# A hybrid decoder layer: POOL's arithmetic given to DVE, the scaling of attention weights to ACT

## The chip, the core and the metric

The kernel runs on one core of one Trainium2 chip. The core has a matrix engine (TensorE, in profiles PE, with its weight loads as PEld), two engines for elementwise work that matter here, VectorE (DVE) and GpSimd (POOL), one for functions and copies, ScalarE (ACT), and a sync engine (SP) whose queue issues the DMAs. The engines run at the same time, each works through its own list of instructions strictly in order, and they wait for each other by semaphores. PE writes its results to PSUM banks, which DVE and ACT read; everything else lies in SBUF, and weights, inputs and results in HBM. The metric is the device time of one execution in microseconds (us).

## What is computed

One layer of a decoder (model width 1024) for a prompt of 2048 positions and 8 sample rows of one position each, which share all weights. In short:

```python
h = rms_norm(x, norm1_w);  proj = h @ w_in
q, k, v, z, xbc, dt_raw = split(proj)
a     = sliding_window_attention(q, k, v, sinks, rel_bias)      # window 128, 8 heads, 2 key/value heads
s_out = ssm_mixer(z, xbc, dt_raw, ...)                          # convolution, chunked state scan, gate, norm
x = x + concatenate([a, s_out]) @ w_out
h2 = rms_norm(x, norm2_w)
x = x + (silu(h2 @ w_gate) * (h2 @ w_up)) @ w_down              # hidden width 2816
y = rms_norm(x, final_norm_w)
```

Attention weights are `e / (sum(e) + exp(sink - m))`, computed in blocks of 128 queries against 256 keys. The scan works in chunks of 128 positions and carries a state of 8 heads x 64 x 128. New keys, values, convolution rows and states are outputs too.

## The kernel before

**Groups.** The 2048 + 8 columns are worked in six groups of 2, 3, 3, 3, 3 and 2 blocks of 128 (the last with the 8 sample rows), that is with 256, 384 or 264 columns. Activations stand with features on partitions, so a matmul has a weight tile of 128 x 128 and 256 to 384 moving columns.

**Pairs.** Every matmul of a projection is done three times to keep float32's precision: a number is split into a rounded half `hi` and a remainder `lo`, and `mm3` (L104 inside `mm`) adds hi*hi, hi*lo and lo*hi. Of activations, ACT makes `hi` by a copy, and DVE or POOL the remainder by a subtraction (L339 in `scaled`, L921 in `stage_s`, L1009 in `hid2`, L554 and L482 for keys and values).

**Weights.** `weight` (L210 and around) brings a weight piece of 128 x 512 (for the down projection mostly 128 x 384). The first times it is loaded raw (L206 into `wraw`, four buffers), ACT rounds it (L207), and DVE and POOL by turns subtract (L210); the pair lies in one of five `w2` buffers. At a first, second or third use, spread over the pieces, the pair is written to HBM (L214), and later uses load it whole (L203). So raw pieces, and with them L207 and L210, are frequent early and end around 1350 us.

**Stages.** Generators emit the work of a stage piece by piece: `stage_x0`/`stage_x` (load and first norm), `stage_a`, `stage_k`, `stage_b` (input projection, convolution), `stage_p` (attention), `stage_q` (state scan, `ssd`), `stage_y` (sample rows), `stage_s` (pairs of the mixed output), `stage_o` (output projection), `stage_h` (second norm), `stage_f` (feed-forward), `stage_z` (final norm, output). `run` advances a main stage and beside it others at set rates, so that the mixers of group i+1 are emitted among the feed-forward of group i. The tile framework then decides by an own estimate of every instruction's time, at build, in which order the instructions stand on each engine; buffers of a tag are taken in turn.

**POOL's work** in this kernel: half of the weight remainders (L210), the squares of the first group (L301), the sums of squares of the norms (`total`, L321), half of the activation remainders (L339, L921, L1009), all remainders of values (L482) and keys (L554), the scaling of attention weights by the inverse denominator (`scale`, L603), the triangular mask of one half (L626), the group sums (L673), three products of the scan (L742, L750, L757), the products and sums of the sample states (L893, L895), and small copies (L403, L407, L462 and others).

Of the kernel before, what the change touches and what calls it, by code (L numbers as in the profile page):

```python
# [31 lines left out]
NH = 8  # L32
# [40 lines left out]
def hymba(ctx: ExitStack, tc: tile.TileContext, I: dict, O: dict, groups):  # L73
# [125 lines left out]
    def weight(name, at, w=512):  # L199
        t = T([P, 1024], F32R, tag="w2", bufs=5)[:, :2 * w]  # L200
        hi, lo = t[:, :w], t[:, w:]
        if (name, at) in kept:
            SP.dma_start(t.bitcast(F32), kept[name, at])  # L203
            return hi, lo
        raw = T([P, 512], tag="wraw", bufs=4)[:, :w]
        SP.dma_start(raw, I[name][at] if name != "wd" else I[name][:, at:at + w])  # L206
        S.activation(hi, raw, AF.Copy)  # L207
        e = G if wn[0] % 2 else V
        wn[0] += 1
        e.tensor_tensor(lo, raw, hi.bitcast(F32), ALU.subtract)  # L210
# [70 lines left out]
    def stage_x0(g):  # L281
# [18 lines left out]
        for m in range(KT):  # L300
            G.tensor_tensor(xr[:, m, :N], xr[:, m, :N], xr[:, m, :N], ALU.mult)  # L301
            if m:
                V.tensor_tensor(xr[:, 0, :N] if m < KT - 1 else r, xr[:, 0, :N], xr[:, m, :N], ALU.add)
            if m % 4 == 3:
                yield
# [13 lines left out]

    def total(sq, t, N, e=G):  # L320
        e.tensor_tensor(sq[:, :N], sq[:, :N], t[:, :N], ALU.add)  # L321
# [11 lines left out]
    def scaled(x, c, r, N, pair, to):  # L333

        ts = {}

        def low(m):
            e = G if m % 2 else V
            e.tensor_tensor(pair[1][:, m, :N], ts[m], pair[0][:, m, :N].bitcast(F32), ALU.subtract)  # L339

        for m in range(KT + 2):
            if m >= 2:
                low(m - 2)
            if 1 <= m <= KT:
                S.activation(pair[0][:, m - 1, :N], ts[m - 1], AF.Copy)
            if m < KT:
                ts[m] = to(m)
                V.scalar_tensor_tensor(ts[m], x[:, m, :N], col(c, m), r[:, :N], ALU.mult, ALU.mult)  # L348
            yield
# [103 lines left out]
    def stage_k(g):  # L453
# [16 lines left out]
        def rows():  # L470
# [8 lines left out]
            for i, src in enumerate((vf[:, 0:nb], vd[:, :nb])):  # L479
                src = src.rearrange("p b (v c) -> p b v c", v=2)  # L480
                S.activation(vs[:, i, :nb, :, 0:64], src, AF.Copy)
                G.tensor_tensor(vs[:, i, :nb, :, 64:P], src, vs[:, i, :nb, :, 0:64].bitcast(F32), ALU.subtract)  # L482
            if last:
# [48 lines left out]
    def attention(g, b):  # L532
# [67 lines left out]
        def scale(kv):  # L600
            for r in range(4):
                h = kv * 4 + r
                G.tensor_scalar(sc[kv][:, r, 0:P], sc[kv][:, r, 0:P], rd[:, h:h + 1], 1.0, ALU.mult, ALU.mult)  # L603

# [11 lines left out]
        def finish(kv):  # L616
# [37 lines left out]
    def stage_q(g):  # L654
# [49 lines left out]
    def ssd(g, b):  # L704
# [68 lines left out]
    def stage_y(g):  # L773
# [111 lines left out]
        for i in range(NS):  # L885
# [6 lines left out]
            V.tensor_tensor(f4(xb), bb(bcb, 0), f4(dx[:, 1, :, i:i + 1].broadcast_to([P, 4, P])), ALU.mult)  # L892
            G.tensor_tensor(h, h, dx[:, 0, :, i:i + 1].broadcast_to([P, 4, P]), ALU.mult)  # L893
            yield
            G.tensor_tensor(h, h, xb, ALU.add)  # L895
            SP.dma_start(O["nss"][:, i], h)
# [15 lines left out]
    def stage_s(g):  # L912
# [6 lines left out]
        def low(t):  # L919
            e = G if t % 2 else V  # L920
            e.tensor_tensor(mix[1][:, t, :N], src[t], mix[0][:, t, :N].bitcast(F32), ALU.subtract)  # L921
# [28 lines left out]
    def norm_sum(g, x1, sq, m, N, n=1):  # L950
# [6 lines left out]
        def second():  # L957
            if m:
                total(sq, t[0], N, V if g is gs[-1] and n == 0 else G)
            g["nsq"] = g.get("nsq", 0) + 1  # L960
# [15 lines left out]
    def stage_f(g):  # L976
# [30 lines left out]
        def hid2(f, t, hh, hl):  # L1007
            e = G if f % 2 else V
            e.tensor_tensor(hl[:, 0, :N], t[:, :N], hh[:, 0, :N].bitcast(F32), ALU.subtract)  # L1009
# [214 lines left out]
```

## Time and profile before

| | |
|---|---|
| runs, us | 2434.94, 2443.29, 2444.47 (median 2443.29) |
| profiled execution, us | 2437.1, its span 2434.7 |
| mean granted clock of PE | 0.985 |
| busy in the span, us | PE 2314.5, weight loads 2244.4, DVE 1250.4, ACT 875.1, POOL 814.4 |
| DMA | 629 MB moved, 258 GB/s on average |

The profile is one execution; its times are of that execution alone. "Busy" is the time in which an engine had an instruction in work; PE's matmuls are pipelined, so that a busy PE need not be at its peak. A slice is a fortieth of the span (61 us), and a digit in it the busy share in tenths. A group of instructions is given as line, engine, operation, written and read tiles (buffer numbers left out), shape and count, then busy us and mean ns of one, then the idle time of the engine just before them and what ended it. A wait is given as who waited for whom, total us, times and longest. In a timeline row the first number is the start, the second the length.

### The profile page before, as it was taken

How to read it: one execution, taken by the hardware profiler on the slowest of the kernel's cores; microseconds unless marked ns; L12 is line 12 of the kernel's file. 1: busy time of each engine (PE TensorE's matmuls, PEld its weight loads, DVE VectorE, ACT ScalarE, POOL GpSimd, SP SyncE). 2: the span in 40 equal slices, each digit the busy share in tenths (PEclk: the TensorE clock that was granted, in tenths of full speed). 3: DMA queues.
4: the chain of work that ended last, by engine and by line, in shares of the span. 5: the costliest groups of instructions: out<-in, count | busy, mean ns of one | idle time of the engine just before them, and what ended most of it. 6: DMA issues, size and time to landing. Idle time of an engine off the chain costs nothing.

```text
span 2434.7 us, 39664 instructions
## 1 busy us (share of the span) xinstructions
PE 2314.5 (95%) x14633; PEld 2244.4 (92%) x14633; DVE 1250.4 (51%) x2526; ACT 875.1 (36%) x1861; POOL 814.4 (33%) x884
## 2 busy tenths in 40 slices
PE   6889898999999999999999999999999999999997
PEld 5779887889999999999999999999989999999997
DVE  8895978564556545344653533453354544233223
ACT  5665556454434434333432422132233212121001
POOL 5555766553444434223322312231123132111000
PEclk9899998999999999999999999999999999999999
DMA  8648575787776777878788887777789788888997
GB/s 276 221 151 284 186 239 195 248 306 272 252 247 212 243 246 278 272 262 277 242 281 285 269 250 243 238 215 240 237 308 301 230 280 270 249 294 306 332 339 259
DMA packets 227227, 628.97 MB, mean 258 GB/s; under 512 B 24323, under 2 KB 57916, under 8 KB 226892
## 3 DMA queue, kind: packets, MB, share of 16 engines
q1 hardware_dynamic: 226892, 626.26, 77.5%
q8 instruction: 116, 1.90, 0.3%
q14 instruction: 75, 0.61, 0.1%
q10 hardware_dynamic: 144, 0.20, 0.0%
HBM read 516.67 MB, written 110.21 MB: 257 GB/s over the span
## 4 chain that ended last, share of the span: by engine, by line
PE 68%; DMA 7%; DVE 2%; ACT 1%; issue 0%; SPq 0%; ACTq 0%; POOL 0%; DVEq 0%
PE psd L104 64%; PE psm L104 4%; DMA w<-wd 2%; DMA w<-wi 2%; DMA w<-wu 1%; DMA w<-wg 1%; DVE x L1042 1%; DVE xr L348 1%; DVE alo L339 0%; DMA out_yT_dram<-x 0%; DMA m<-sbcd 0%; PE psm L608 0%; PE psm L728 0%; DVE w L210 0%; ACT L696 0%
## 5 line engine op out<-in xcount | busy, mean ns | idle before, releaser
L104 PE MATMUL psd<-bhi,w 128*128 128x384 f32 (+1 forms) x4448 | 1097.4, 328 | 40.0 <-DVE w L210 14.9
L104 PEld LDWEIGHTS psd<-bhi,w 128*128 128x128 f32 x4448 | 785.6, 190 | 54.6 <-DVE w L210 19.1
L104 PE MATMUL psd<-blo,w 128*128 128x384 f32 (+1 forms) x2224 | 720.8, 324 | 0.7 <-DVE blo L339 0.6
L104 PE MATMUL psd<-hc,w 128*128 128x384 f32 (+2 forms) x3168 | 527.5, 323 | 28.6 <-DMA w<-wd 9.8
L104 PEld LDWEIGHTS psd<-hc,w 128*128 128x128 f32 x3168 | 502.5, 191 | 43.3 <-issue 12.4
L104 PE MATMUL psd<-ahi,w 128*128 128x384 f32 (+1 forms) x2272 | 516.7, 314 | 22.4 <-DMA w<-wi 8.4
L104 PEld LDWEIGHTS psd<-blo,w 128*128 128x128 f32 x2224 | 423.2, 190 | 2.8 <-DVE blo L339 1.1
L104 PEld LDWEIGHTS psd<-ahi,w 128*128 128x128 f32 x2272 | 386.1, 189 | 31.2 <-DMA w<-wi 5.0
L210 POOL TENSOR_TENSOR w<-wraw,w 128x512 fp32r<-128x512 f32 (+1 forms) x195 | 252.7, 1298 | 382.1 <-ACT w L207 346.3
L104 PE MATMUL psd<-alo,w 128*128 128x384 f32 (+1 forms) x1136 | 354.9, 312 | 0.0
L207 ACT ACTIVATE w<-wraw 128x512 fp32r<-128x512 f32 (+1 forms) x391 | 232.5, 601 | 324.4 <-PE psd L104 187.7
L994 DVE TENSOR_TENSOR x<-psd,x 128x384 f32<-128x384 f32 (+2 forms) x336 | 168.0, 510 | 193.9 <-PE psd L104 193.4
L104 PEld LDWEIGHTS psd<-alo,w 128*128 128x128 f32 x1136 | 215.2, 189 | 1.3
L210 DVE TENSOR_TENSOR w<-wraw,w 128x512 fp32r<-128x512 f32 (+1 forms) x196 | 164.4, 840 | 90.7 <-ACT w L207 88.6
L1009 POOL TENSOR_TENSOR hc<-tmp,hc 128x384 fp32r<-128x384 f32 (+2 forms) x66 | 67.6, 1025 | 356.8 <-ACT hc L1005 356.7
L1001 DVE SCALAR_TENSOR_TENSOR tmp<-tmp,psd 128x384 f32<-128x384 f32 (+2 forms) x132 | 66.7, 505 | 233.2 <-ACT tmp L1015 233.0
L1015 ACT ACTIVATE tmp<-psd 128x384 f32<-128x384 f32 (+2 forms) x132 | 59.7, 452 | 349.4 <-PE psd L104 349.2
L321 POOL TENSOR_TENSOR sq<-sq,tmp 128x384 f32<-128x384 f32 (+2 forms) x112 | 109.7, 979 | 199.4 <-ACT tmp L318 194.4
L1004 DVE SCALAR_TENSOR_TENSOR tmp<-psd,tmp 128x384 f32<-128x384 f32 (+2 forms) x132 | 67.4, 511 | 199.1 <-PE psd L104 198.8
L1005 ACT ACTIVATE hc<-tmp 128x384 fp32r<-128x384 f32 (+2 forms) x132 | 64.4, 488 | 270.4 <-DVE tmp L1004 267.0
L382 DVE SCALAR_TENSOR_TENSOR x<-tmp,cols,x 128x384 f32<-128x384 f32 (+1 forms) x144 | 100.3, 700 | 37.2 <-ACT x L404 26.7
L318 ACT ACTIVATE tmp<-x 128x384 f32<-128x384 f32 (+2 forms) x84 | 40.5, 489 | 137.5 <-DVE x L942 100.4
(269 smaller groups left out, 2145.3 us busy)
## 6 DMA issues: line engine op xcount, KB each, us to landing
w<-wu SPq DMA_DIRECT2D x177, 512.0 KB, 5.0
w<-wg SPq DMA_DIRECT2D x175, 512.0 KB, 4.5
w<-wi SPq DMA_DIRECT2D x144, 512.0 KB, 4.6
w<-wd SPq DMA_DIRECT2D x192, 384.0 KB, 3.8
w<-wo SPq DMA_DIRECT2D x65, 512.0 KB, 4.6
wraw<-in_wg_dram SPq DMA_DIRECT2D x89, 256.0 KB, 4.3
wu<-w SPq DMA_DIRECT2D x44, 512.0 KB, 3.3
wg<-w SPq DMA_DIRECT2D x44, 512.0 KB, 3.7
```

Source lines behind the costliest of these rows:

```text
L104: PE.matmul(o, l, r, start=start, stop=stop)
L207: S.activation(hi, raw, AF.Copy)
L210: e.tensor_tensor(lo, raw, hi.bitcast(F32), ALU.subtract)
L318: S.activation(t[:, :N], x[:, m, :N], AF.Square)
L321: e.tensor_tensor(sq[:, :N], sq[:, :N], t[:, :N], ALU.add)
L382: V.scalar_tensor_tensor(acc, raw[:, j:j + NP], cwc(j, t), acc, ALU.mult, ALU.add)
L994: V.tensor_tensor(x1[:, m, :N], p[:, :N], x1[:, m, :N], ALU.add)
L1001: V.scalar_tensor_tensor(t[:, :N], t[:, :N], 1.0, pg[:, :N], ALU.add, ALU.mult)
L1004: V.scalar_tensor_tensor(t[:, :N], pu[:, :N], 0.5, t[:, :N], ALU.mult, ALU.mult)
L1005: S.activation(hh[:, 0, :N], t[:, :N], AF.Copy)
L1009: e.tensor_tensor(hl[:, 0, :N], t[:, :N], hh[:, 0, :N].bitcast(F32), ALU.subtract)
L1015: S.activation(t[:, :N], pg[:, :N], AF.Tanh, scale=0.5)
```

## The change

All tensor_tensor instructions of POOL (G in the code: sums, differences and products) are issued on DVE (V) instead, with the same operands. Where the two engines took turns, DVE takes all. The scaling of the attention weights, four tensor_scalar instructions per key/value head, becomes four ACT copies with a scale per partition. POOL keeps its copies and memsets. One line falls away in `weight`, so that from there on the line numbers of the changed kernel are lower by one (L210 becomes L209).

```diff
 def weight(name, at, w=512):
         S.activation(hi, raw, AF.Copy)
-        e = G if wn[0] % 2 else V
-        wn[0] += 1
+        e = V
         e.tensor_tensor(lo, raw, hi.bitcast(F32), ALU.subtract)
...
 def stage_x0(g):
-            G.tensor_tensor(xr[:, m, :N], xr[:, m, :N], xr[:, m, :N], ALU.mult)
+            V.tensor_tensor(xr[:, m, :N], xr[:, m, :N], xr[:, m, :N], ALU.mult)
...
-    def total(sq, t, N, e=G):
+    def total(sq, t, N, e=V):
         e.tensor_tensor(sq[:, :N], sq[:, :N], t[:, :N], ALU.add)
...
         def low(m):
-            e = G if m % 2 else V
+            e = V
...
-                G.tensor_tensor(kl[r, kv, :W], kT[a, (b + k0) * P:(b + 2) * P], kh[a, kv, :W].bitcast(F32), ALU.subtract)
+                V.tensor_tensor(kl[r, kv, :W], kT[a, (b + k0) * P:(b + 2) * P], kh[a, kv, :W].bitcast(F32), ALU.subtract)
...
         def scale(kv):
             for r in range(4):
                 h = kv * 4 + r
-                G.tensor_scalar(sc[kv][:, r, 0:P], sc[kv][:, r, 0:P], rd[:, h:h + 1], 1.0, ALU.mult, ALU.mult)
+                S.activation(sc[kv][:, r, 0:P], sc[kv][:, r, 0:P], AF.Copy, scale=rd[:, h:h + 1])
...
-                G.tensor_tensor(as4(own[0]), as4(f32(ph)), tri4, ALU.mult)
+                V.tensor_tensor(as4(own[0]), as4(f32(ph)), tri4, ALU.mult)
...
-            G.tensor_tensor(s0[:, :N], s0[:, :N], s1[:, :N], ALU.add)
+            V.tensor_tensor(s0[:, :N], s0[:, :N], s1[:, :N], ALU.add)
...
 def ssd(g, b):
-        G.tensor_tensor(xdd, xdt, sm[:, 1, :].unsqueeze(2).broadcast_to([P, NH, 64]), ALU.mult)
+        V.tensor_tensor(xdd, xdt, sm[:, 1, :].unsqueeze(2).broadcast_to([P, NH, 64]), ALU.mult)
...
-        G.tensor_tensor(state, state, sm[:, 0, :].unsqueeze(2).broadcast_to([P, NH, 64]), ALU.mult)
+        V.tensor_tensor(state, state, sm[:, 0, :].unsqueeze(2).broadcast_to([P, NH, 64]), ALU.mult)
...
-            G.tensor_tensor(e, e, cb[:, q, :].unsqueeze(1).broadcast_to([P, 4, P]), ALU.mult)
+            V.tensor_tensor(e, e, cb[:, q, :].unsqueeze(1).broadcast_to([P, 4, P]), ALU.mult)
...
         def hid2(f, t, hh, hl):
-            e = G if f % 2 else V
+            e = V
```

Left out are the same replacement at L482, L893, L895, L921 and in `norm_sum`, where an exception for the last group becomes the rule.

The order of the instructions moves with it. Names in the rows carry buffer numbers, the last number being the tile's own.

First place: the first projection of the first group, where `blo` is the remainder of its input, `xr` the input that is squared (L301) and summed (L303), and `w2` a weight half out of `wraw`. Before, on DVE:

```order
L298 SCALAR_TENSOR_TENSOR blo_14_82<-xr_15_83,cols_4_68,bhi_13_81 128x256
L210 TENSOR_TENSOR w2_24_160<-wraw_25_161,w2_24_160 128x512
L303 TENSOR_TENSOR xr_15_83<-xr_15_83 128x256
L150 COPY m2_20_121<-psm_18_117 8x384
L475 COPY m2_128_702<-vp_11_77 128x128
L210 TENSOR_TENSOR w2_32_202<-wraw_33_203,w2_32_202 128x512
```

The second half of the first weight, w2_27_166, is not among these rows; it stands on POOL, between squares:

```order
L301 TENSOR_TENSOR xr_15_83<-xr_15_83 128x256 x7
L210 TENSOR_TENSOR w2_27_166<-wraw_28_167,w2_27_166 128x512
L301 TENSOR_TENSOR xr_15_83<-xr_15_83 128x256
L210 TENSOR_TENSOR w2_34_207<-wraw_35_208,w2_34_207 128x512
L210 TENSOR_TENSOR w2_40_247<-wraw_41_248,w2_40_247 128x512
```

Now, on DVE, from the same remainder on:

```order
L297 SCALAR_TENSOR_TENSOR blo_14_82<-xr_15_83,cols_4_68,bhi_13_81 128x256
L300 TENSOR_TENSOR xr_15_83<-xr_15_83 128x256
L209 TENSOR_TENSOR w2_24_160<-wraw_25_161,w2_24_160 128x512
L300 TENSOR_TENSOR xr_15_83<-xr_15_83 128x256
L302 TENSOR_TENSOR xr_15_83<-xr_15_83 128x256
L150 COPY m2_20_121<-psm_18_117 8x384
L209 TENSOR_TENSOR w2_27_166<-wraw_28_167,w2_27_166 128x512
```

Squares and both halves of the weight stand in one list, the second half behind the first.

Second place: the feed-forward of the first group, with the mixers of the second emitted among it; `x1` is the residual sum that empties a PSUM bank (L994), `sm` small sums of attention. Before, on DVE:

```order
L210 TENSOR_TENSOR w2_665_3703<-wraw_666_3704,w2_665_3703 128x512
L994 TENSOR_TENSOR x1_375_2135<-psd_656_3650,x1_375_2135 128x256
L210 TENSOR_TENSOR w2_674_3754<-wraw_675_3755,w2_674_3754 128x512
L994 TENSOR_TENSOR x1_375_2135<-psd_659_3666,x1_375_2135 128x256
L994 TENSOR_TENSOR x1_375_2135<-psd_662_3682,x1_375_2135 128x256
```

One half per weight stands here, its neighbour on POOL. Now, on DVE:

```order
L209 TENSOR_TENSOR w2_665_3703<-wraw_666_3704,w2_665_3703 128x512
L209 TENSOR_TENSOR w2_668_3709<-wraw_669_3710,w2_668_3709 128x512
L993 TENSOR_TENSOR x1_375_2135<-psd_656_3650,x1_375_2135 128x256
L581 TENSOR_SCALAR sm_680_3794<-sm_680_3794 128x8
L582 TENSOR_TENSOR sm_680_3794<-cols_4_68,sm_680_3794 128x8
L993 TENSOR_TENSOR x1_375_2135<-psd_659_3666,x1_375_2135 128x256
L209 TENSOR_TENSOR w2_674_3754<-wraw_675_3755,w2_674_3754 128x512
```

Both halves of a weight stand one behind the other ahead of the evacuation, and the attention's small sums have come in between the evacuations.

More of the change, by code (lines that the diff above doesn't have):

```diff
@@ L481, in rows @@
                 S.activation(vs[:, i, :nb, :, 0:64], src, AF.Copy)
-                G.tensor_tensor(vs[:, i, :nb, :, 64:P], src, vs[:, i, :nb, :, 0:64].bitcast(F32), ALU.subtract)
+                V.tensor_tensor(vs[:, i, :nb, :, 64:P], src, vs[:, i, :nb, :, 0:64].bitcast(F32), ALU.subtract)
             if last:
@@ L892, in stage_y @@
             V.tensor_tensor(f4(xb), bb(bcb, 0), f4(dx[:, 1, :, i:i + 1].broadcast_to([P, 4, P])), ALU.mult)
-            G.tensor_tensor(h, h, dx[:, 0, :, i:i + 1].broadcast_to([P, 4, P]), ALU.mult)
+            V.tensor_tensor(h, h, dx[:, 0, :, i:i + 1].broadcast_to([P, 4, P]), ALU.mult)
             yield
-            G.tensor_tensor(h, h, xb, ALU.add)
+            V.tensor_tensor(h, h, xb, ALU.add)
             SP.dma_start(O["nss"][:, i], h)
@@ L919, in low @@
         def low(t):
-            e = G if t % 2 else V
+            e = V
             e.tensor_tensor(mix[1][:, t, :N], src[t], mix[0][:, t, :N].bitcast(F32), ALU.subtract)
@@ L958, in second @@
             if m:
-                total(sq, t[0], N, V if g is gs[-1] and n == 0 else G)
+                total(sq, t[0], N, V)
             g["nsq"] = g.get("nsq", 0) + 1
@@ L1007, in hid2 @@
         def hid2(f, t, hh, hl):
-            e = G if f % 2 else V
+            e = V
             e.tensor_tensor(hl[:, 0, :N], t[:, :N], hh[:, 0, :N].bitcast(F32), ALU.subtract)
```

## The prediction, made before the changed kernel ran

> **What bounds the kernel now.** I read the page first (busy shares, then the slices), then busy time by stages, then TensorE's waits in the early stage, then the groups of that stage on DVE and POOL.
>
> ```profile
> PE 2314.5 (95%) x14633; PEld 2244.4 (92%) x14633; DVE 1250.4 (51%) x2526; ACT 875.1 (36%) x1861; POOL 814.4 (33%) x884
> PE   6889898999999999999999999999999999999997
> DVE  8895978564556545344653533453354544233223
> POOL 5555766553444434223322312231123132111000
> ```
>
> Over the whole span PE is busy 95%, so neither DVE nor POOL can be the bound on average. The slices show where that average misleads: PE's digits under 9 lie in the first eight slices (61 us each), and there DVE stands at 8, 8, 9, 5, 9, 7, 8, 5 and POOL at 5 to 7.
>
> ```profile
> 0.00:500.00 500.00, 429.82 (x2994) 396.15 (x2994) 379.48 (x711) 284.74 (x611) 293.14 (x299) 0.96 0.69 227
> 600.00:2435.00 1835.00, 1788.70 (x11084) 1754.66 (x11082) 819.30 (x1720) 547.25 (x1168) 478.21 (x534) 0.99 0.80 265
> ```
>
> Columns: stretch, length, busy us of PE, weight loads, DVE, ACT, POOL, then granted clock, DMA share, GB/s. In the first 500 us PE is idle 70 us and its granted clock is 0.96; in the last 1835 us it is idle 46. What ends the idle time is different in the two parts. TensorE's longest waits, first of the first 600 us, then of the rest:
>
> ```profile
> PE psd L104 <- DVE w L210: 15.6, 14, 3.1
> PE psd L104 <- ACT w L207: 10.4, 10, 2.6
> PE psd L104 <- POOL w L210: 8.5, 12, 1.7
> PE psd L104 <- DVE x L994: 8.3, 5, 2.5
> ```
> ```profile
> PE psd L104 <- DMA w<-wd: 9.8, 11, 2.2
> PE psd L104 <- DMA w<-wi: 8.4, 7, 2.2
> PE psd L104 <- DMA w<-wu: 6.6, 6, 1.5
> ```
>
> Early, PE waits for the split of fresh weights (ACT's rounded half at L207, then the remainder at L210 on DVE or POOL by turns) and for DVE to empty PSUM banks (L994). Late, it waits for weight loads alone, 24.8 us in these three rows. The DMA queue on SP repeats the early story, since a raw load may only start when an earlier split has freed one of the four raw buffers (waits of the first 600 us):
>
> ```profile
> SPq L206 <- POOL w L210: 81.2, 53, 7.0
> SPq L206 <- DVE w L210: 76.4, 31, 8.2
> ```
>
> So the change decides in the first 500 us, where DVE and POOL set how fast weights arrive.
>
> **What the two engines cost each other.** Three rows of the timeline, one split beside POOL's, one alone:
>
> ```profile
> 11.51 1.44 POOL L210 TENSOR_TENSOR w<-wraw,w 128x512 fp32r<-128x512 f32 x1
> 11.75 1.75 DVE L210 TENSOR_TENSOR w<-wraw,w 128x512 fp32r<-128x512 f32 x1
> 15.40 0.68 DVE L210 TENSOR_TENSOR w<-wraw,w 128x512 fp32r<-128x512 f32 x1
> ```
>
> The same DVE instruction takes 1.75 us when POOL works and 0.68 when it doesn't. In the groups of the first 500 us this is a rule for operations whose tensors all lie in SBUF, and absent where one is a PSUM bank (L994):
>
> ```profile
> L210 DVE TENSOR_TENSOR w<-wraw,w 128x512 fp32r<-128x512 f32 x85 | 74.5, 878 | 49.3 <-ACT w L207 48.8
> L210 DVE TENSOR_TENSOR w<-wraw,w 128x384 fp32r<-128x384 f32 x24 | 23.6, 984 | 8.3 <-ACT w L207 8.2
> L738 DVE TENSOR_SCALAR big<-big,cs 128x128 f32<-128x128 f32 x40 | 21.6, 604 | 0.5 <-ACT m L720 0.5
> L382 DVE SCALAR_TENSOR_TENSOR x<-tmp,cols,x 128x384 f32<-128x384 f32 x24 | 20.5, 859 | 0.7 <-POOL tmp L403 0.4 <-ACT x L404 0.2
> L382 DVE SCALAR_TENSOR_TENSOR x<-tmp,cols,x 128x256 f32<-128x256 f32 x24 | 18.4, 777 | 1.8 <-ACT x L404 1.5
> L994 DVE TENSOR_TENSOR x<-psd,x 128x256 f32<-128x256 f32 x48 | 18.7, 413 | 2.0 <-PE psd L104 1.9
> L348 DVE SCALAR_TENSOR_TENSOR xr<-xr,cols,sq 128x384 f32<-128x384 f32 x16 | 17.0, 1129 | 0.0
> L760 DVE SCALAR_TENSOR_TENSOR m<-x,cols,m 128x128 f32<-128x128 f32 x20 | 14.4, 772 | 0.0
> ```
>
> Undisturbed prices come from the whole span's rows of these lines (shortest / median / longest ns):
>
> ```profile
> L210 DVE TENSOR_TENSOR w<-wraw,w x196: 537/693/2348, 11.8 to 1350.3; 128x512 fp32r<-128x512 f32 x148, 128x384 fp32r<-128x384 f32 x48
> L738 DVE TENSOR_SCALAR big<-big,cs x128: 329/337/1452, 98.6 to 1904.6; 128x128 f32<-128x128 f32 x128
> L382 DVE SCALAR_TENSOR_TENSOR x<-tmp,cols,x x144: 462/612/1725, 27.0 to 1822.1; 128x384 f32<-128x384 f32 x96, 128x256 f32<-128x256 f32 x48
> L348 DVE SCALAR_TENSOR_TENSOR xr<-xr,cols,sq x40: 484/618/1621, 73.8 to 1633.7; 128x384 f32<-128x384 f32 x32, 128x264 f32<-128x264 f32 x8
> L760 DVE SCALAR_TENSOR_TENSOR m<-x,cols,m x64: 333/344/1393, 106.1 to 1915.9; 128x128 f32<-128x128 f32 x64
> ```
>
> The Trainium skill (SBUF — State Buffer, SBUF: two separate sides) says that DVE and GpSimd hold one pair of SBUF ports in turn, exclusively and for a whole instruction, when the DVE instruction has two SBUF inputs or runs in a two-port mode. The trace agrees: 878 against 693 ns at L210, no inflation at L994 (413). By that rule the whole inflation goes with POOL's arithmetic. If the long DVE rows came from something else, the 79 us given back below would stay, and even at 93% the stage would take 545 us.
>
> **The change part by part, first 500 us.** POOL's groups there, the two largest and the one that goes to ACT:
>
> ```profile
> L210 POOL TENSOR_TENSOR w<-wraw,w 128x512 fp32r<-128x512 f32 x84 | 116.0, 1383 | 98.2 <-ACT w L207 91.2 <-PE psm L104 4.2 <-DVE w L210 1.8
> L210 POOL TENSOR_TENSOR w<-wraw,w 128x384 fp32r<-128x384 f32 x24 | 26.0, 1089 | 25.6 <-ACT w L207 19.7 <-DVE hc L1009 5.7 <-POOL alo L339 0.2
> L603 POOL TENSOR_SCALAR big<-big,sm 128x128 f32<-128x128 f32 x40 | 21.4, 553 | 12.9 <-ACT w L207 12.0 <-DVE sm L593 0.8
> ```
>
> *Added to DVE.* Of POOL's 293 us, 21 are the scaling; I count the other 272 as moved, with the few small copies that stay. DVE does a 512-wide one in 0.69 instead of 1.383 us and a 384-wide one in 0.54 instead of 1.089: half, so 136 us. Neighbours on DVE overlap a little (48 times 413 ns at L994 are 19.8 us, the group is busy 18.7), which makes it 128.
>
> *Given back on DVE.* L210: 85 x (878 - 693) = 15.7 and 24 x (984 - 537) = 10.7; L738: 40 x (604 - 337) = 10.7; L382: 24 x (859 - 612) = 5.9 and, against its shortest, 24 x (777 - 462) = 7.6; L348: 16 x (1129 - 618) = 8.2; L760: 20 x (772 - 344) = 8.6. Sum 67. Smaller groups of the same kind I take at 12, an estimate at the same proportion.
>
> *DVE's need* is then 379 + 128 - 67 - 12 = 428 us for what takes 500 us now: 86% of it instead of 76%. POOL's 293 us fall to copies. The price of the move is thus 49 us on an engine with 120 idle, and what decides is how well DVE's queue can be kept busy. From both sides: two stretches of before show what it reaches.
>
> ```profile
> 60.00:120.00 60.00, 49.67 (x347) 44.65 (x345) 48.59 (x95) 37.09 (x85) 33.63 (x35) 0.89 0.66 219
> 240.00:300.00 60.00, 52.15 (x398) 47.09 (x396) 55.86 (x105) 35.24 (x82) 46.36 (x44) 1.00 0.57 188
> ```
>
> 81% in the first, 93% in the second. 428 us at 93% are 460 (40 less than now), at 86% 500 (nothing), at 81% 528 (28 more). I take 89%, 481 us, **19 less**. Nearer to 93 than to 81, because the largest idle of DVE today is 58 us in front of its own L210 (49.3 and 8.3, ACT still rounding), and the moved instructions give the queue other work to stand there; not at 93, because behind a split that waits for ACT now stands everything: PSUM evacuations (L994), which PE waits for, and the other split, which SP waits for. A split on POOL ends 0.69 us later than one on DVE that starts at once, so a DVE wait up to 0.69 us longer than POOL's still loses nothing there.
>
> *The scaling on ACT.* 128 instructions leave POOL. The nearest row on ACT has the same shape and an operand per partition:
>
> ```profile
> L588 ACT ACTIVATE big<-big,sm 128x128 f32<-128x128 f32 x8 | 3.1, 387 | 0.0
> ```
>
> 40 of them in the first 500 us are 15.5 us on an engine with 215 idle; four in a row take 1.55 us instead of 2.2 on POOL. In front of a rounding at L207 they cost up to 1.55 us, ten times: bounds 0 and 15.5, taken as 0, since ACT is idle 43% there. The Trainium skill (ScalarE: Activation LUTs, Rules for kernel authors) speaks against this part: products belong on VectorE. By the same page (What ACT_TABLE_LOAD costs) an estimate for one pointer operand is 0.39 us, as in the row; on DVE at L738's 337 ns the 40 would be 13.5 us more in the crowded queue, so here the rule would lose.
>
> **After 500 us.** PE has no time to win from splits there. What remains are loads that stand in SP's queue behind work of DVE; the chain of waits around 790 us:
>
> ```profile
> 784.46 6.53 DVE xr L348 x8
> 792.21 3.95 DVE alo L339 x3
> 797.92 7.64 DMA w<-wd
> ```
>
> The eight L348 shrink from 6.53 to about 8 x 0.6 = 4.9 us; L339 doubles on DVE from four to eight but halves in price. That is 1.6 us earlier for the load behind them, of which PE, mostly covered there, sees little: **1 less** (bounds 0 and 5, three such places).
>
> **Order.** The build's own estimate sets every engine's order. At the two places shown with the change, the second split of the first projection no longer runs beside the first but behind it and a square, and in the feed-forward two splits precede a PSUM evacuation that had one: 0.69 us more if both are ready, and a wait for ACT twice. Both count against a higher share than 89%.
>
> **Sum.** The profiled execution took 2437.1 us (span 2434.7). 2437.1 - 19 - 1 = 2417. The median of the three runs is 6 us above it; I name 2420, between that and 2443 - 20.
>
> **Rivals.** *DVE's queue becomes the bound* (slower): DVE can't be kept over 81%, because L210 waits for ACT at its head while evacuations and the next splits stand behind; raw loads then start later, and the first 500 us take 528, so 2465; at today's 76% it would be 563 and 2500. It decides below 86%. For it: the waits on DVE's own L210 above; against it: the 93% stretch, and that the cross-engine price goes. *A wash*: 86%, the relief just pays for the load, 2437 to 2443. *The loads are the bound anyway*: splits come sooner, but the four raw buffers then wait for DMA (share 0.69 in this stage), so only PE's own 8.5 us behind POOL's splits go: 2429 to 2435. Against it: 158 us of waits of L206 for splits. That the change doesn't do what it says I exclude, the arithmetic has left POOL's list.
>
> **Chances.** Forecast 0.47; DVE's queue 0.25; wash 0.20; loads 0.08. What differs by under 0.5% (12 us) of 2443 can't be told from no change. Faster takes the forecast and a part of the loads case, 0.50; slower most of the queue case, 0.23; same 0.27. The range: 93% gives 2437 - 40 - 5 = 2392, the queue case 2465; I take 2390 to 2465. The forecast's own range is 2395 to 2431.
>
> **What would show it.** In the changed kernel's profile: L209 at 512 wide near 0.69 us throughout; L737 near 337 and L759 near 344 ns; DVE's share in the first 500 us above 86%; PE's waits for POOL gone and those for DVE's splits not above the 24 us that both have now; the 1800 us behind within some us. I am wrong if DVE's share stays near 80%, with waits for L209 and L993 grown, or if DVE's rows stay long without POOL.

## The result, and the profile after

The changed kernel took 2375.95 us (median of 4 runs, 2370.76 to 2380.70), the kernel before beside it 2443.88 (4 runs): a ratio of 0.9728, 95% interval 0.9697 to 0.9760. Two later sets of runs gave 0.9753 (0.9732 to 0.9775) and 0.9758 (0.9739 to 0.9777). The gain is 68, 58 and 61 us in the three sets and 59.5 between the spans of the two profiled executions, some 60 us where the forecast named 23; the forecast's direction holds, its size doesn't, and 2376 lies below its range.

The page of the changed kernel, busy shares and slices:

```profile
span 2375.2 us, 39240 instructions
...
PE 2290.4 (96%) x14633; PEld 2230.5 (94%) x14633; DVE 1382.0 (58%) x3173; ACT 911.8 (38%) x1989; POOL 31.5 (1%) x109
...
PE   7999998999999999999999999999999999999997
...
DVE  8987978665778555366745535554455574233223
...
POOL 1000000000000000000000000000000000000000
```

POOL is nearly empty. PE's early digits, which were 6889898 at first, are now 7999998. And DVE, which took over POOL's arithmetic, has grown from 1250.4 to 1382.0 us, 132 more for 783 that left POOL, of which the scaling, 53.5 us, went to ACT.

How much time the first stage lost can be read from the stage view, where PE's count of matmuls tells how far the program has come. Before, then after, at the same count (columns as in the prediction: stretch, length, then busy us of PE, weight loads, DVE, ACT, POOL, granted clock, DMA share, GB/s):

```profile
0.00:494.00 494.00, 424.50 (x2957) 391.54 (x2958) 375.84 (x706) 280.05 (x601) 289.23 (x295) 0.96 0.68 226
...
600.00:2435.00 1835.00, 1788.70 (x11084) 1754.66 (x11082) 819.30 (x1720) 547.25 (x1168) 478.21 (x534) 0.99 0.80 265
```
```profile
0.00:450.00 450.00, 405.01 (x2956) 381.41 (x2957) 378.02 (x925) 291.32 (x642) 15.68 (x38) 0.98 0.75 248
...
600.00:2375.00 1775.00, 1738.28 (x10800) 1704.89 (x10798) 911.96 (x2047) 550.28 (x1212) 12.85 (x54) 1.00 0.81 267
```

The changed kernel reaches the 2957th matmul at 450 us instead of 494: **44 us of the gain arise there**. DVE needs 378 us to get there, as before 376, with 219 instructions more. The rest of the gain, 15 us (59.5 between the two spans, less 44), is spread over the 1925 us behind. PE is idle 36.7 us in the last 1775 where it was idle 46.3 in the last 1835.

The rows that the prediction wanted to see. Undisturbed prices over the whole kernel (shortest / median / longest ns), then the groups of the first 452 us:

```profile
L209 DVE TENSOR_TENSOR w<-wraw,w x391: 535/683/696, 11.0 to 1294.9; 128x512 fp32r<-128x512 f32 x148, 128x384 fp32r<-128x384 f32 x48
L737 DVE TENSOR_SCALAR big<-big,cs x128: 335/341/347, 86.6 to 1847.2; 128x128 f32<-128x128 f32 x128
L759 DVE SCALAR_TENSOR_TENSOR m<-x,cols,m x64: 334/343/348, 96.9 to 1858.9; 128x128 f32<-128x128 f32 x64
```
```profile
L209 DVE TENSOR_TENSOR w<-wraw,w 128x512 fp32r<-128x512 f32 x167 | 113.1, 685 | 34.9 <-ACT w L207 34.2
L209 DVE TENSOR_TENSOR w<-wraw,w 128x384 fp32r<-128x384 f32 x48 | 25.9, 551 | 7.9 <-ACT w L207 7.7
L993 DVE TENSOR_TENSOR x<-psd,x 128x256 f32<-128x256 f32 x48 | 19.0, 414 | 0.3 <-PE psd L104 0.3
...
L347 DVE SCALAR_TENSOR_TENSOR xr<-xr,cols,sq 128x384 f32<-128x384 f32 x16 | 8.6, 612 | 0.0
```

The long tails are gone: the longest split took 2348 ns before and takes 696 now. TensorE's waits in the first 500 us, then in the rest from 600 us on:

```profile
PE psd L104 <- DVE w L209: 12.3, 16, 2.0
PE psd L104 <- DVE tmp L362: 8.0, 1, 8.0
PE psd L104 <- ACT w L207: 7.7, 11, 1.3
...
PE psd L104 <- DVE x L993: 2.7, 3, 1.5
```
```profile
PE psd L104 <- DMA w<-wi: 6.9, 6, 3.0
...
PE psd L104 <- DMA w<-wd: 3.9, 6, 1.5
PE psd L104 <- DMA w<-wu: 3.9, 6, 1.4
```

Waits for splits cost PE 12.3 us where they cost 15.6 and 8.5; the evacuation L993 2.7 where it cost 8.3. The three late rows for weight loads fell from 24.8 to 14.7 us. One wait has grown from 1.4 to 8.0 us, that for L362 (L363 before) between 20 and 30 us: there `got_dt` multiplies by the row of the first normalisation, whose squares now stand in DVE's list. L362 starts at 28.4 us where it started at 25.5; the rest of the longer wait is that TensorE arrives there earlier. The raw loads in the DMA queue wait for splits less than before, 104.2 us in the first 500 against 80.7 + 76.4 in the same stretch of before:

```profile
SPq L206 <- DVE w L209: 104.2, 78, 6.3
```

### The profile page after: what moved, and what is told of

The parts are those of the page before. It is cut to its first block, busy times and chain, and to the rows that moved or that the text cites. A ratio compares the mean times of both kernels' runs of the same rounds, so it can differ in the third digit from the quotient of the medians.

```text
span 2375.2 us, 39240 instructions
## 1 busy us (share of the span) xinstructions
PE 2290.4 (96%) x14633; PEld 2230.5 (94%) x14633; DVE 1382.0 (58%) x3173; ACT 911.8 (38%) x1989; POOL 31.5 (1%) x109
## 4 chain that ended last, share of the span: by engine, by line
PE 77%; DMA 11%; DVE 6%; ACT 3%; issue 2%; SPq 0%; ACTq 0%; DVEq 0%
PE psd L104 72%; PE psm L104 5%; DVE w L209 2%; DMA w<-wi 2%; DMA w<-wg 1%; DMA w<-wu 1%; DMA w<-wd 1%; DMA wraw<-in_wu_dram 1%; DMA wraw<-in_wg_dram 1%; ACT w L207 1%; DMA wraw<-in_wd_dram 1%; DMA wraw<-in_wi_dram 1%; ACT big L587 0%; DMA wraw<-in_wo_dram 0%; PE psm L607 0%
## 5 line engine op out<-in xcount | busy, mean ns | idle before, releaser
L104 PE MATMUL psd<-hc,w 128*128 128x384 f32 (+2 forms) x3168 | 521.4, 321 | 15.6 <-DMA w<-wd 3.9
L104 PEld LDWEIGHTS psd<-hc,w 128*128 128x128 f32 x3168 | 496.8, 188 | 25.8 <-DVE w L209 5.2
L209 DVE TENSOR_TENSOR w<-wraw,w 128x512 fp32r<-128x512 f32 (+1 forms) x391 | 252.9, 653 | 101.8 <-ACT w L207 98.3
L993 DVE TENSOR_TENSOR x<-psd,x 128x384 f32<-128x384 f32 (+2 forms) x336 | 168.5, 510 | 132.8 <-PE psd L104 132.1
L381 DVE SCALAR_TENSOR_TENSOR x<-tmp,cols,x 128x384 f32<-128x384 f32 (+1 forms) x144 | 80.5, 567 | 37.9 <-ACT x L403 23.2
L1008 DVE TENSOR_TENSOR hc<-tmp,hc 128x384 fp32r<-128x384 f32 (+2 forms) x132 | 67.6, 512 | 29.4 <-ACT hc L1004 29.3
L320 DVE TENSOR_TENSOR sq<-sq,tmp 128x384 f32<-128x384 f32 (+2 forms) x119 | 61.5, 517 | 34.9 <-ACT tmp L317 33.8
L587 ACT ACTIVATE big<-big,sm 128x256 f32<-128x256 f32 (+1 forms) x128 | 62.4, 489 | 20.8 <-DVE sm L581 20.6
```

Of the source, the lines that this page charges most:

```text
L104: PE.matmul(o, l, r, start=start, stop=stop)
L381: V.scalar_tensor_tensor(acc, raw[:, j:j + NP], cwc(j, t), acc, ALU.mult, ALU.add)
L587: S.activation(sc[kv][:, r, :W], sc[kv][:, r, :W], AF.Exp, bias=ng[:, h:h + 1], accum_out=den[:, h:h + 1])
L993: V.tensor_tensor(x1[:, m, :N], p[:, :N], x1[:, m, :N], ALU.add)
```

## The experiments

Three theories stood against each other at first. *Contention*: POOL's arithmetic stretched those DVE instructions whose tensors lie in SBUF, and that is what the change took away. *Lateness*: POOL made every second split in 1.38 us where DVE takes 0.69, so the remainder and the raw buffer came late. *Order*: the build puts DVE's list in a better order when POOL is out of it. All ratios below are against the kernel before on the same chip, with 95% intervals; line numbers of kernels built on the changed one are one lower than those of before.

**e1 and e2: half the change each.** e1 is the kernel before with the splits alone given to DVE, e2 everything but the splits.

```
e1 (on before)                          e2 (on the changed kernel)
-        e = G if wn[0] % 2 else V      -        e = V
-        wn[0] += 1                     +        wn[0] += 1      (ahead of the load)
+        e = V                          +        e = V if wn[0] % 2 else G
```

> The kernel before with one part of the change: all weight splits (L210) on DVE, everything else of POOL stays there. Contention theory (the gain is DVE's own instructions shortened, because POOL's arithmetic no longer holds the ports that two-operand SBUF instructions need): POOL keeps about 69% of its 814 us (the splits are 253 of them), so DVE gets only about a third of its relief back while it takes over 130 us: 2410 to 2440. Latency theory (the gain is that a split on POOL took 1.38 us and on DVE 0.69, so weights arrive sooner): nearly the whole gain, 2376 to 2390.

> The changed kernel with the weight splits again by turns on POOL and DVE; everything else of the change stays. Contention theory: POOL works 250 us instead of 814, nearly all of it before 500 us, so about a third of the stretching returns, and DVE is relieved of 125 us: 2385 to 2405. Latency theory: most of the gain is gone, 2420 to 2440.

e1: 2403.12 us (2401.18 to 2410.34), ratio 0.9881 (0.9852 to 0.9909), 30 less. e2: 2406.31 us, 0.9889 (0.9864 to 0.9914), 27 less. Neither theory met both: e1 lies between the two ranges expected for it, e2 just above contention's and well below latency's. Each half is worth about half, and they add up (57 of some 60). Their places differ:

```profile
0.00:461.00 461.00, 412.68 (x2959) 387.71 (x2960) 381.95 (x814) 281.77 (x602) 159.90 (x189) 0.96 0.72 243
```
```profile
0.00:478.00 478.00, 415.34 (x2957) 390.25 (x2958) 375.60 (x817) 292.88 (x644) 154.39 (x145) 0.95 0.69 234
```

The first row is e1's, the second e2's: the same work is done at 461 us with the splits moved (33 us less than before) and at 478 with the rest moved (16 less). By the whole spans (2399.1 and 2405.2 against 2434.7) e1 gains 2 to 3 us more to the end and e2 13. So the late 15 us of the change come with the work that isn't a split, the early 44 with both. In both POOL still works a third of the time, and the 512-wide split on DVE takes 762 ns on average in e1 and 778 in e2, between 878 and 685.

**e3 and e7: the small parts.** e3 is the changed kernel with the scaling of attention weights back on POOL (`G.tensor_scalar` instead of `S.activation`, 128 instructions); e7 has POOL's remaining small copies (L402, L406, L461, `G.tensor_copy` to `V.tensor_copy`) on DVE as well.

> The changed kernel with the scaling of attention weights back on POOL (128 instructions of about 0.4 us). Contention theory: POOL works 50 us more of 2375, and one-operand instructions at that: within 5 us of the changed kernel, 2371 to 2381. If the scaling on ACT is itself what pays (POOL's place in the attention chain): 2385 or more.

> The changed kernel with POOL's small copies of the convolution's history (L402, L406) and of the last keys (L461) on DVE too; POOL has no work left until the sample rows. Contention theory: 102 copies of some 0.3 us on POOL cost little either way, 2370 to 2382. It is the base for two further runs, in which POOL gets work of its own again.

e3: 2381.89 us, 0.9788 (0.9762 to 0.9813); e7: 2379.35, 0.9788 (0.9755 to 0.9821). On that chip the changed kernel didn't run. Of its ratios elsewhere, e7's interval overlaps all three, e3's the two later ones (0.9753 and 0.9758) and just misses the first (0.9728). e3 has both small parts on POOL and e7 neither, and on the one chip they differ by 2.5 us, so the two together are worth no more than some us. e3 lies 1 us above the range of contention and under the 2385 of its rival. One scaling on ACT takes 388 ns, as in the row that the prediction used (387):

```profile
L602 ACT ACTIVATE big<-big,sm x128: 382/388/411, 111.1 to 1989.8; 128x128 f32<-128x128 f32 x128
```

e7 is useful as a base: nearly nothing stands on POOL in it, so that POOL can be loaded at will.

**e4 and e5: POOL busy again, with reads or with writes.** On e7, a tile of its own (128x256) that nobody else uses is worked on by POOL from the start: 330 products in e4, 1000 memsets in e5. The order of the instructions on TensorE, DVE, ACT and SP is the same in e4, e5 and e7.

```
+    pb = T([P, 256], tag="scp")
+    G.memset(pb, 1.0)                           (e4)
+    for _ in range(330):
+        G.tensor_tensor(pb, pb, pb, ALU.mult)
                                                 (e5: 1000 times G.memset(pb, 1.0))
```

> The changed kernel with its small copies on DVE, and 330 extra additions to POOL's list: in-place products of a private tile of 128x256, one after the other from the start, which nobody waits for. The instructions of all other engines stand in the same order as without them. Latency theory and order theory (the gain is a better order of DVE's list): no change, 2370 to 2385. Contention theory: POOL works some 270 us without a pause; the first 270 us of DVE's two-operand SBUF rows are stretched as before or more (splits of 512 from 0.69 to 0.9 us and over, L737 from 0.34 to 0.6), which by the 105 us that 293 us of POOL cost DVE before are some 95 us of DVE; the time grows by 40 to 95 us, 2420 to 2475.

> The same with 1000 memsets of that tile on POOL in place of the products: POOL only writes. If what DVE loses is lost to POOL's reading of SBUF, two-operand splits stay at 0.69 us and only one-operand SBUF instructions (L737) may stretch: within 10 us of the kernel without them, 2370 to 2390. If any instruction of POOL does it: as with the products, 2420 or more.

e4: 2454.72 us, 1.0072 (1.0050 to 1.0093), slower than before. e5: 2378.24, 0.9761 (0.9741 to 0.9781), the changed kernel's time. Three groups of e4 in the first 280 us and the row of its stage to the 2964th matmul, then the same two views of e5:

```profile
L209 DVE TENSOR_TENSOR w<-wraw,w 128x512 fp32r<-128x512 f32 x77 | 68.0, 896 | 6.4 <-ACT w L207 6.3
L381 DVE SCALAR_TENSOR_TENSOR x<-tmp,cols,x 128x384 f32<-128x384 f32 x24 | 19.9, 830 | 0.0
...
L737 DVE TENSOR_SCALAR big<-big,cs 128x128 f32<-128x128 f32 x16 | 11.0, 749 | 0.0
```
```profile
0.00:530.00 530.00, 433.56 (x2964) 402.52 (x2965) 475.94 (x959) 293.79 (x642) 269.50 (x335) 0.92 0.63 212
```
```profile
L209 DVE TENSOR_TENSOR w<-wraw,w 128x512 fp32r<-128x512 f32 x101 | 68.1, 683 | 16.3 <-ACT w L207 16.0
L381 DVE SCALAR_TENSOR_TENSOR x<-tmp,cols,x 128x384 f32<-128x384 f32 x24 | 14.5, 606 | 0.3 <-ACT x L403 0.2
...
L737 DVE TENSOR_SCALAR big<-big,cs 128x128 f32<-128x128 f32 x32 | 9.3, 417 | 0.0
```
```profile
0.00:454.00 454.00, 410.44 (x2959) 387.23 (x2960) 380.56 (x959) 291.07 (x642) 313.88 (x1004) 0.97 0.73 247
```

The same 959 DVE instructions take 476 us beside POOL's products and 381 beside its memsets, though POOL is busy longer with the latter (314 us against 270). All of it lies in DVE's rows without a PSUM operand: matched one by one with e7, they take 97 us more in e4, those with a PSUM operand 97 us in both, and ACT's 642 instructions 329 us in both. The 512-wide split goes from 683 to 896 ns beside products and stays at 683 beside memsets; of these three groups only L737, which reads one large tensor of SBUF, feels memsets too (417 ns, 341 in the changed kernel). POOL's products on a tile that nobody waits for cost 75 us against e7, 76 against e5 on the same chip. This is contention by itself, and with the order held fixed order can't be the main cause: the time is bad with e7's order and good with it. The Trainium skill (SBUF — State Buffer, SBUF: two separate sides) says the same, that a DVE instruction with two SBUF inputs contends only with a GpSimd instruction that reads SBUF, one in a two-port mode with any; the trace agrees with the first half (683 ns in e5 as in e7 for the split). L737's 417 against 341 would fit the second, but no trace shows in which mode it runs.

**e12: the stretch near before's share.** In e4 the products fill 91% of POOL's time for 296 us, which before never did: its POOL arithmetic filled 56% of the first 494 us. e12 puts two memsets behind each of the 330 products, in e7's order again; the products then fill 49% of POOL's time over 538 us (0.55 over 470 had been expected).

> e4 with two memsets of POOL behind each of the 330 products on the private tile, so that the products fill about 0.55 of POOL's time for some 470 us instead of 0.96 for 280, much as POOL's work did in before; order on the other engines as in e7. Stretch theory: DVE's rows L209 (512 wide) near 0.80 us and L381 near 0.72 us over the first 450 us, DVE's busy time to the same work up by 80 to 110 us, time 40 to 80 us above e7, 2419 to 2459. If the stretch costs nothing below e4's share: under 2400.

Two groups of its DVE, then the stage, with e7's below it:

```profile
L209 DVE TENSOR_TENSOR w<-wraw,w 128x512 fp32r<-128x512 f32 x140 | 105.4, 763 | 17.3 <-ACT w L207 14.7 <-PE psm L104 2.1
...
L381 DVE SCALAR_TENSOR_TENSOR x<-tmp,cols,x 128x384 f32<-128x384 f32 x24 | 17.3, 722 | 0.0
```
```profile
0.00:502.00 502.00, 425.90 (x2957) 393.73 (x2958) 448.20 (x958) 293.01 (x642) 441.23 (x924) 0.95 0.67 223
...
0.00:453.00 453.00, 407.25 (x2964) 383.76 (x2965) 380.54 (x959) 291.48 (x643) 0.20 (x4) 0.98 0.74 248
```

2429.40 us (2426.15 to 2431.14), 0.9969 (0.9957 to 0.9980): 50 more than e7, which ran on another chip (44 by the ratios), and nearly the time of before. The size was met in time (40 to 80) and a little under in DVE's busy time (68 us more, 80 to 110 expected). The groups above are those of the first 450 us, the rows below them the stage. A stretch of 68 us on DVE takes away most of what the change won.

**e6: DVE loaded without any stretch.** The changed kernel with one more DVE product (128x256, on the private tile) behind each of the 391 splits.

```
         e.tensor_tensor(lo, raw, hi.bitcast(F32), ALU.subtract)
+        V.tensor_tensor(pb, pb, pb, ALU.mult)
```

> The changed kernel with one more DVE instruction behind each weight split, an in-place product of a private tile of 128x256 (0.41 us, 391 of them, 215 in the first 452 us: 88 us more on a DVE that is busy 379 of 452). If DVE is the bound of that stage, all that does not fit in its 73 idle us and a part of the rest is paid: 2420 to 2470. If DVE has slack there and what counts is only how soon a split is done: up to 20 us, 2376 to 2396.

The added products over the whole kernel, and the stage:

```profile
L210 DVE TENSOR_TENSOR scp<-scp 128x256 f32<-128x256 f32 x391 | 163.3, 418 | 2.8
```
```profile
0.00:485.00 485.00, 417.74 (x2960) 391.18 (x2961) 450.16 (x1147) 292.02 (x642) 17.52 (x38) 0.95 0.69 230
```

2414.23 us, 0.9908 (0.9881 to 0.9936), 38 more than the changed kernel beside it (2376.70). Nearly all of it arises early: the point of the 2960th matmul comes 35 us later for 72 us more of DVE, about half a us for each. The other 91 of the 163 us, later in the kernel, cost 3. The time lies between the two ranges expected (2420 to 2470, 2376 to 2396), and the build reorders DVE's list here too, so that half a us is the price of both.

**e9 and e11: lateness without reads.** e9: behind every split POOL overwrites 256 columns of the raw buffer, so that the next raw load waits for POOL. e11: behind every second split POOL overwrites the remainder (which is thus left out of the products for half the weights) and eight columns of the raw buffer, so that PE and the load both wait for POOL. The build reorders the lists somewhat in both.

```
e9   +        G.memset(raw[:, 0:256], 0.0)
e11  +        wn[0] += 1
     +        if wn[0] % 2:
     +            G.memset(lo.bitcast(F32), 0.0)
     +            G.memset(raw[:, 0:8], 0.0)
```

> The changed kernel with one memset of POOL behind each of the 391 splits, over the first 256 columns of the raw buffer just read: nothing is computed from it, but the buffer comes free 0.8 us later or more (a POOL memset of that size took 0.81 us), as it did when POOL made every second split. DVE's splits are not stretched by memsets (683 ns beside them, 684 without). Turnaround theory (part of the gain is that raw buffers come free sooner, since DVE splits in 0.69 us where POOL took 1.38): 15 to 40 us more than the changed kernel, 2391 to 2416, all of it in the first 450 us. Contention alone: 2374 to 2382, the changed kernel's time. The order on the engines differs somewhat from the changed kernel's, since the build counts the memsets.

> The changed kernel, but behind every second split POOL overwrites the remainder just made (512 columns) with zeros and eight columns of the raw buffer, so that TensorE and the next raw load wait for POOL as they did for its own splits: by e9's 0.31 us for 256 columns, about 0.65 us and one handing over later. The remainder of half the weights is thus left out of the products. POOL reads nothing from SBUF and DVE still makes all splits. Lateness theory (e9: 10 us for 0.31 us behind every split): 10 to 30 us more than the changed kernel, 2386 to 2406. If lateness is nothing by itself and only the stretch counts: 2373 to 2382.

e9: 2385.53 us, 0.9798 (0.9781 to 0.9816), 10 more than the changed kernel beside it (2375.29). The 0.81 us per memset in its expectation is the time of one of e4's products (815 ns); a memset of that size took 313 ns, so the buffers came free only 0.31 us and a handing over later, and the result lies below the 15 to 40 expected and outside contention alone. e11: 2393.82 us, 0.9827 (0.9810 to 0.9845), 18 more than the 2376 of the changed kernel on other chips (17 by the ratios), as lateness wanted (10 to 30). Its memset on the remainder and the stage:

```profile
L212 POOL MEMSET w<- 128x512 f32 x148 | 78.1, 528 | 794.7 <-DVE w L209 530.2 <-issue 118.1 <-PE psd L104 51.7
```
```profile
0.00:465.00 465.00, 413.86 (x2960) 386.91 (x2961) 380.11 (x925) 291.19 (x642) 71.37 (x252) 0.97 0.71 241
```

DVE's need is the changed kernel's (380 us), its share falls from 84% to 82%, and the stage is 15 us longer. So lateness looks like a cause of its own, smaller than the stretch; but how much of the 18 is the changed order was not tried.

**e10: the same products where DVE has room.** e4's 330 products, held back by a tile that DVE fills behind the first group's feed-forward.

```
+        if g is gs[0]:                          (stage_z, ahead of rinv_b)
+            pb = T([P, 256], tag="scp")
+            V.tensor_scalar(pb, sq[:, :256], 0.0, 1.0, ALU.mult, ALU.add)
+            for _ in range(330):
+                G.tensor_tensor(pb, pb, pb, ALU.mult)
```

> The kernel of e7 with the same 330 POOL products on a private tile as in e4, but held back until the last normalisation of the first group (about 800 us), by a tile that DVE fills there; order on TensorE, ACT and SP as in e7, DVE one instruction more. Contention theory with slack late: DVE's rows with two SBUF operands in those 270 us stretch as in e4 (L381 near 0.8 us, L737 near 0.75 us) and its busy share there rises by 0.15 or more, but the time goes up by 0 to 15 us only (2378 to 2394), because DVE is idle half of that stage. Rival (POOL's products slow the kernel by something else, a clock or a DMA, wherever they stand): 50 to 80 us more, as in e4, 2430 to 2460.

2404.49 us, 0.9872 (0.9854 to 0.9890), 25 more than e7: neither the 0 to 15 of contention with slack nor the 50 to 80 of the rival. The products began at 470 us, not at 800, since the tile that they wait for was filled that early. The stretch from 495 to 750 us of e7, then of e10:

```profile
495.00:750.00 255.00, 254.07 (x1512) 250.48 (x1511) 168.81 (x370) 117.49 (x247) 0.00 (x0) 1.00 0.72 247
```
```profile
495.00:750.00 255.00, 240.65 (x1370) 234.31 (x1371) 214.65 (x354) 102.23 (x215) 231.29 (x298) 0.97 0.67 229
```

DVE was at 66% there, not at half, and rises to 84% while doing 354 instructions instead of 370; its rows stretch as in e4 (L381 858 ns, L737 752). Room of a third isn't enough to hide such a stretch, though it cuts the cost of the same 330 products from 75 us to 25.

**e8: a further step.** The squares of the first normalisation on ACT (`S.activation(..., AF.Square)` at L300), for the 8.0 us wait on L362.

> The changed kernel with the squares of the first normalisation (L300, eight in all) taken from DVE to ACT. Occupancy theory (an early us of DVE costs about 0.5 us, and TensorE waits 8.0 us for the last of that chain, L362 at 21 to 29 us): about 3 us off DVE and part of the 8.0 us wait go, 2 to 8 us less than the changed kernel, 2368 to 2374 beside its 2376. Rival (the chain ends with the sums on DVE, and the first weights wait as before): the changed kernel's time within 2 us. If ACT, which now rounds weights behind the squares, is late: up to 5 us more.

2381.68 us (2377.99 to 2383.77), 0.9779 (0.9761 to 0.9797), 6 more than the changed kernel beside it and nearest to the last of the three cases expected. TensorE's waits in the first 500 us of the changed kernel in that set, then of e8:

```profile
PE psd L104 <- DVE w L209: 10.5, 17, 2.0
PE psd L104 <- ACT w L207: 7.4, 11, 1.3
PE psd L104 <- DVE tmp L362: 7.1, 1, 7.1
```
```profile
PE psd L104 <- DVE w L209: 12.2, 19, 1.5
PE psd L104 <- ACT w L207: 11.1, 12, 2.7
...
PE psd L104 <- DVE tmp L362: 2.4, 1, 2.4
```

The wait on L362 shrinks by 4.7 us, and the waits for ACT's rounding (3.7 more) and for splits (1.7 more) take it back; that ACT's first roundings are late behind eight squares would fit this. These rows leave 1 of the 6 us, the rest isn't explained. No version that ran beats the changed kernel.

The changed kernel itself, run again beside them:

> The changed kernel itself once more, on the same chip as the runs beside it: 0.97 to 0.976 of the kernel before, as the first time.

> The changed kernel once more, beside the three on the same chip: 2371 to 2381 us, the ratio between 0.970 and 0.978 by all theories.

2376.70 and 2375.29 us, as given with the result.

## Why the prediction came out as it did

**Right: the place and the mechanism.** The first 500 us decide (44 of 59.5 us), DVE and POOL set the pace there, and POOL's arithmetic was what made DVE's rows long. The prices came out as named: 685 ns for L209 at 512 (0.69 forecast), 341 for L737 (337), 343 for L759 (344), 612 for L347 (618). PE's waits for POOL are gone, those for splits are 12.3 us against the bound of 24.

**Not contradicted: the scaling on ACT at 0.** e3 and e7 differ by 2.5 us, and e3's interval resolves no difference from the two later sets of the changed kernel.

**Wrong: DVE's need.** The prediction's step "379 + 128 - 67 - 12 = 428" should have come to about 381: at the same work DVE's need is 378.0 us, against 375.8 before. The stretch being 494 us rather than 500 is worth 4 us of that; the rest are three mis-sized terms, found by matching the groups of both traces up to the 2957th matmul. First, 12 for the smaller groups was an estimate and came to 37: the sum of all that was given back is 104 us. The seven groups that were counted gave 67, as forecast, but L338, L1008, L627, L677 and some dozens of groups with a few tenths of a us to 4 us each had been stretched too (two of them below, before and after). Second, the moved work came to 127 us, not 136; of the 272 us that were halved, 12 were the copies that stay on POOL. Third, neighbours on DVE overlap more when the list is denser: the rows add up to 439.9 us for 378.0 busy (61.9 overlapped), before to 417.1 for 375.8 (41.3). That is 21 us where 8 had been allowed. Together 25 + 9 + 13 = 47 us. The price of moving 127 us of work onto DVE was thus about 2 us of DVE's time, not 49.

```profile
L339 DVE TENSOR_TENSOR alo<-xr,ahi 128x384 fp32r<-128x384 f32 x8 | 8.5, 1087 | 0.0
L628 DVE TENSOR_TENSOR m<-m,cst 128x512 fp32r<-128x512 f32 x8 | 7.5, 937 | 0.1
```
```profile
L338 DVE TENSOR_TENSOR alo<-xr,ahi 128x384 fp32r<-128x384 f32 x16 | 8.3, 548 | 0.0
...
L627 DVE TENSOR_TENSOR m<-m,cst 128x512 fp32r<-128x512 f32 x8 | 5.4, 679 | 0.0
```

**Wrong, in the other direction: the share.** 89% had been chosen; it was 378/450 = 84%, under the 86% that had been named as a sign. Taken with the right need, 89% would have given 425 us, 69 less; at 84% it is 450, 44 less. The two errors offset each other: the prediction's own 428 us at the 84% that came would have taken 510 us, longer than before. That it named the right direction is in part luck. The share is not a property of the queue, as the prediction took it: in the runs it mostly rises with the need, and at equal need with splits that come in time. DVE is busy 93% in e6 (450 us of 485), 90% in e4, 89% in e12, and 84% here, where with less work on DVE part of its idle time is spent in front of splits that ACT hasn't rounded yet (34.9 and 7.9 us in the rows of L209). At nearly the same need it was 76% before, 79% in e2 with half the splits on POOL and 83% in e1 with all of them on DVE; that POOL's late splits keep it down fits these three, though in e11 it falls to 82% only. So the bounds from 81% to 93% held the share, but multiplied a need that was too large. The rivals rested on the same need: *DVE's queue becomes the bound* and *a wash* took 81% and 86% of 428 us. *The loads are the bound anyway* fell too: the DMA brought the same 112 MB to that point at 248 GB/s where before had 226, so it hadn't been at its limit.

**Missed: lateness.** The prediction used POOL's slow split only as a margin ("a DVE wait up to 0.69 us longer than POOL's still loses nothing"), and put none of it into the sum. e11 puts 18 us on about that lateness, whatever its changed order adds included. With the 50 us of e12 for the stretch this makes 68, of which the moved work costs a part, and some 60 remain. The three don't add up: extra load on DVE cost half a us per us in e6, which for 127 us of moved work would be 63, where 68 less 60 leaves 8. The stretch of e12, 68 us of DVE's time, is also smaller than the 104 us in the rows that fell away. What the same load costs depends on what else holds the stage up, and I can't split the 44 us further from these runs.

**Mis-sized: after 500 us.** "1 less" was about 12: when the changed kernel stood at 495 us, it was 48 us ahead of before, at the end 60. The eight L347 of the chain shrink as forecast (6.53 to 4.32 us in one such place of the timeline, 4.9 forecast), and PE's waits for weight loads fell by 10 us in the three rows; that these belong together isn't shown place by place. The bound of 5 had been taken from three places of one chain, and the reading that TensorE waits late for weight loads alone left out some 4 us of small waits for DVE and ACT. e1 and e2 put the late gain on the work other than splits, and e10 shows that the stage from 495 to 750 us isn't as insensitive as its PE share of 99% suggests: 231 us of POOL's products there cost some 23.

**Order.** The rows that front the prediction counted against a higher share, and DVE's list does have the second split behind the first. What can be seen of a cost is L362, which starts 3 us later than before, and which no term had.

## What to carry to other kernels

Before giving work to POOL or taking it away, compare the mean and the shortest duration of every DVE group that has its tensors in SBUF, the small ones too: where they differ, POOL's work is paid for twice, and its removal may be nearly free for DVE although it does everything then. Make the sum from all groups and from busy time at an equal count of matmuls; the largest groups held only two thirds of what was given back here. An engine at 66% in a stage where TensorE is busy 99% still has less room than these numbers suggest.

## What the runs showed of the hardware that was not expected

POOL's memsets cost DVE's two-operand instructions nothing (683 ns with POOL 84% busy in e5), while its products make the same instruction 896 ns.

The granted clock of TensorE moved roughly with the pauses. It is 0.985 over the span before and 0.994 after, 0.96 and 0.98 in the stretches to the 2957th matmul, and 0.92 in e4, where PE waits most; PE's busy time for those matmuls fell from 424.5 to 405.0 us while its idle time fell from 69.5 to 45.0. So 19.5 of the 44 us came with a shorter busy time for the same matmuls, which no term of the prediction had; how much of it is the clock and how much weights that were there in time the runs don't separate. The Trainium skill (TensorE: Matmul & The Clock Gate, Part 1: The HAM clock gate) has the clock throttled by default and released by activity; the direction in these six stretches agrees by and large (0.92 in e4 with 96 us idle, 0.95 in e12 with 76 and in e6 with 67, 0.96 before with 70, 0.97 in e5 with 44, 0.98 after with 45).
